# Griffin layer on one core: three tiles for r, i and the states of a chain step, and another place for the squared decay

## The chip, the core and the metric

The kernel runs on one core of a Trainium2 chip, in float32. The metric is the device time of one execution in microseconds (us). TensorE (PE) multiplies, ScalarE (ACT) runs activations and copies, VectorE (DVE) elementwise work and the scans, GpSimd (POOL) and SyncE (SP) issue DMA transfers. Each engine works through its own list of instructions in order; across engines they wait on semaphores.

## What is computed

One Griffin layer on 1024 tokens of width 2048, then a gated embedding. Cut to what matters (`proj[..., :2048]` is the branch that is convolved, the other half the gate):

```python
u = rmsnorm(h, norm_pre)
proj = u @ w_in                              # 2048 -> 4096
xb, gate = proj[..., :2048], proj[..., 2048:]
xc = causal_conv_width4(xb, conv_w) + conv_b # per channel
r = sigmoid(blockdiag(xc, w_r) + b_r)        # 8 blocks of 256 channels
i = sigmoid(blockdiag(xc, w_i) + b_i)
log_a = -8 * r * softplus(-lam)
a = exp(log_a)
b = sqrt(-expm1(2 * log_a)) * (i * xc)
h_t = a_t * h_{t-1} + b_t                    # scan over the tokens
y = (h * silu(gate)) @ w_out
h = h + rmsnorm(y, norm_post)
h = h + sigmoid(h @ w_gate) * (p @ w_ple)
```

## The kernel before, in words

**Matrix products.** Channels lie on the 128 partitions and tokens on the free axis, in two halves of 512 tokens (h=0 and h=1). Each float32 product is made of three matmuls of rounded parts (`mm3`): high weight by high operand (line 116), high by low (117), low by high (118). ACT makes a high part by a copy (106), DVE the low part by a subtraction (107). Weights are split so one product ahead of their use, into one of three places (`wp`, names whi_ and wlo_). The three large matrices go by Strassen's scheme: seven products m1 to m7 for each pair of output blocks, each a unit of 24 matmuls. A name such as x14m5 is product m5 of block 14 of w_in. Some weight tiles are sums, which a DMA that adds makes ahead of the product; GpSimd issues it (423).

**Where the chain stands.** While w_in's products run, the recurrent part runs between them, in eight blocks n of 256 channels, for h=0 some 5.4 units apart and for h=1 four products apart. A block has these steps:

- `block_conv`: one ACT instruction for each 128 channels starts xc (280), three DVE instructions each add a tap (283), and xc is split into a high and a low part in the tile x2 (106, 107).
- `block_ri`: one unit of 24 matmuls, r and i of the block, with a weight tile of its own (whi_ri, wlo_ri).
- `chain`: sigmoids for R and I (310, 311), I times xc (312), a tanh into Q (314), an exponential in place of R (318), squared three times: twice in place (319, 320) and once into A2 (321). Then Q = (A2 + 1) * Q on DVE (322), its root on ACT (323), I times Q (324), and the scan (328), which writes the states over Q. For h=0 the states are stored to memory, four units later; for h=1 they are multiplied with the gate into g (335), and g is stored four units later. Sigmoid and tanh, the exponential and the root each need another function table on ACT, so table loads stand between them.

**Places.** The pool named chain has one place for each tag, except two for the tag xb (the convolution's input). xc has 4 KB per partition, x2 8 KB (high and low part), rq 12 KB (R, I and Q in one tile). A2 is written over xc. A tile that takes a place waits until every reader of the tile before it has finished.

**Order.** SP and GpSimd issue in the order of the program text. PE, ACT and DVE get theirs from a scheduler that sees the program's order and the places, so that a change of places can reorder these three. In program order the convolution of block n+1 comes behind chain n for h=0; for h=1 it comes ahead of the matmuls of ri n, because there it is put two products behind a start that moves by four, and the matmuls six.

Of the kernel before, what the change touches and what calls it, by code (L numbers as in the profile page):

```python
# [9 lines left out]
F32R = mybir.dt.float32r  # L10
AF = mybir.ActivationFunctionType
ALU = mybir.AluOpType

P = 128
D = 2048
S = 1024
T = 512
# [17 lines left out]
def trunk_kernel(ctx, tc, xT, pT, par, w_in, w_ri, w_out, w_gate, w_ple, out):  # L35
    nc = tc.nc
# [11 lines left out]
    def bank(name):  # L48
        return psum.tile([P, T], F32, tag="ps", name=name)
# [4 lines left out]
    def chain_tile(tag, name, shape=(P, 2, T), dtype=F32, bufs=1):  # L54

        return pools["a"].tile(list(shape), dtype, tag=tag, name=name, bufs=bufs)
# [16 lines left out]
    def col(base, i):  # L73
        return cst[:, base + i : base + i + 1]
# [30 lines left out]
    def split(hi, lo, src):  # L105
        nc.scalar.activation(hi, src, AF.Copy)  # L106
        nc.vector.tensor_tensor(lo, src, hi.bitcast(F32), ALU.subtract)  # L107
# [7 lines left out]
    def mm3(ps, whi, wlo, ahi, alo, start, stop, more=False):  # L115
        nc.tensor.matmul(ps, whi, ahi, start=start, stop=False, skip_group_check=more)  # L116
        nc.tensor.matmul(ps, whi, alo, start=False, stop=False, skip_group_check=more)  # L117
        nc.tensor.matmul(ps, wlo, ahi, start=False, stop=stop, skip_group_check=more)  # L118
# [36 lines left out]
    st = {}  # L155
# [32 lines left out]
    def put(key, d, src, k=1):  # L188

        n_spills[0] += 1  # L190
        name = f"sp{n_spills[0]}"

        def store():
            t = spill(name, src.shape)
            nc.gpsimd.dma_start(t, src)  # L195
            d[key] = t

        later(k, store)
# [70 lines left out]
    def block_conv(h, n):  # L269
        xbp = st.pop(("xbp", h, n))  # L270
        c = slice(2 * n, 2 * n + 2)
        if h == 0:
            nc.vector.memset(xbp[:, :, 0:3], 0.0)
            nc.vector.tensor_copy(xcar[:, c, :], xbp[:, :, T : T + 3])
        else:
            nc.vector.tensor_copy(xbp[:, :, 0:3], xcar[:, c, :])
        xc = chain_tile("xc", f"xc{h}_{n}")
        for s in range(2):
            ct = 2 * n + s
            nc.scalar.activation(xc[:, s], xbp[:, s, 3 : T + 3], AF.Identity, bias=col(C_CB, ct),  # L280
                                 scale=col(C_CW + 48, ct))
            for j in (2, 1, 0):
                nc.vector.scalar_tensor_tensor(xc[:, s], xbp[:, s, j : j + T], col(C_CW + 16 * j, ct), xc[:, s],  # L283
                                               op0=ALU.mult, op1=ALU.add)
        x2 = chain_tile("x2", f"x2{h}_{n}", (P, 2, 2, T), F32R)
        split(x2[:, 0], x2[:, 1], xc)
        st["xc", h, n], st["x2", h, n] = xc, x2

    def block_ri(h, n):
        plain(w_ri[n], f"ri{h}_{n}", lambda u: mm_ri(h, n, u.pop("w")))  # L290

    def mm_ri(h, n, w):
        hi, lo = w
        x2 = st.pop(("x2", h, n))
        banks = [[bank(f"ri{h}_{n}_{a}{b}") for b in range(2)] for a in range(2)]
        for ri in range(2):
            for dd in range(2):
                for k in range(2):
                    c0 = ri * 512 + k * 256 + dd * P
                    mm3(banks[ri][dd], hi[:, c0 : c0 + P], lo[:, c0 : c0 + P], x2[:, 0, k], x2[:, 1, k],  # L300
                        k == 0, k == 1)
        chain(h, n, banks)

    def chain(h, n, banks):
        rq = chain_tile("rq", f"rq{h}_{n}", (P, 3, 2, T))
        R, I, Q = (rq[:, j] for j in range(3))
        A2 = st.pop(("xc", h, n))
        for s in range(2):
            ct = 2 * n + s
            nc.scalar.activation(R[:, s], banks[0][s], AF.Sigmoid, bias=col(C_BR, ct))  # L310
            nc.scalar.activation(I[:, s], banks[1][s], AF.Sigmoid, bias=col(C_BI, ct))
        nc.vector.tensor_tensor(I, I, A2, ALU.mult)
        for s in range(2):
            nc.scalar.activation(Q[:, s], R[:, s], AF.Tanh, scale=dk[:, 0, 2 * n + s : 2 * n + s + 1])

        for s in range(2):
            ct = 2 * n + s
            nc.scalar.activation(R[:, s], R[:, s], AF.Exp, scale=dk[:, 1, ct : ct + 1])
        nc.scalar.activation(R, R, AF.Square)
        nc.scalar.activation(R, R, AF.Square)  # L320
        nc.scalar.activation(A2, R, AF.Square)
        nc.vector.scalar_tensor_tensor(Q, A2, 1.0, Q, op0=ALU.add, op1=ALU.mult)
        nc.scalar.activation(Q, Q, AF.Sqrt)
        nc.vector.tensor_tensor(I, I, Q, ALU.mult)
        for s in range(2):
            ct = 2 * n + s
            init = 0.0 if h == 0 else hcar[:, ct : ct + 1]
            nc.vector.tensor_tensor_scan(Q[:, s], R[:, s], I[:, s], init, ALU.mult, ALU.add)
        if h == 0:
            nc.vector.tensor_copy(hcar[:, 2 * n : 2 * n + 2], Q[:, :, T - 1])  # L330
            for s in range(2):
                put(2 * n + s, hs, Q[:, s], 4)
        else:
            g = gs.pop(n)
            nc.vector.tensor_tensor(g, Q, g, ALU.mult)  # L335
            for s in range(2):
                put((("b12", "b22")[s], n), yd, g[:, s], 4)
# [484 lines left out]
    for h in range(NH):  # L822
        for n in range(NB):
            o = o2 - 4 + int(5.4 * n) if h == 0 else o3 + 5 + int(4.1 * n)
            if h == 0:
                at(o, lambda n=n: block_load(n))
            at(o + 2, lambda h=h, n=n: block_conv(h, n))
            at(o + 6, lambda h=h, n=n: block_ri(h, n), True)
# [138 lines left out]
```

## Time and profile before

| | us |
|---|---|
| median of 3 runs | 1428.23 |
| lowest and highest of them | 1427.18 and 1430.15 |
| the profiled execution | 1433.68 |
| its span, as the profile shows it | 1431.9 |
| PE busy in it | 1386.0 (97%) |
| DVE, ACT, POOL busy | 975.1, 720.3, 272.5 |

The profiled execution is 5.45 us longer than the median, and 1.78 us of it lie outside the span. The chain in h=0 stands between about 200 and 560 us of the span, the one in h=1 between about 570 and 820. In a row of the timeline, the time in brackets is how long the engine stood idle before it, and the name behind the arrow what ended that. The profile leaves out the numbers in names: x is the high or low part of xc, x0m any product of block 0, rq any block's tile.

### The profile page before, as it was taken

The numbers are of one execution on the slowest core, as the hardware profiler recorded it, in microseconds if no ns is written. First come the engines' busy times: TensorE is split into PE (matmuls) and PEld (weight loads), VectorE is DVE, ScalarE is ACT, GpSimd is POOL, SyncE is SP. The second block draws the span as 40 slices with busy tenths as digits, with TensorE's granted clock in tenths as the row PEclk, the third lists the DMA queues.
The fourth block names the chain that finished last, engine by engine and source line by source line (L and its number), as shares of the span: only waits on it lengthen the run. The fifth ranks groups of instructions, "written<-read, shape, count | busy, mean of one in ns | idle before, by whom it ended". The sixth has DMA issues, their size and how long they took to land.

```text
span 1431.9 us, 17158 instructions
## 1 busy us (share of the span) xinstructions
PE 1386.0 (97%) x6025; PEld 1132.2 (79%) x6025; DVE 975.1 (68%) x1299; ACT 720.3 (50%) x935; POOL 272.5 (19%) x422
## 2 busy tenths in 40 slices
PE   9999898999999999999999989999999999999997
PEld 6888676888888888877777868888787887788886
DVE  7587866666666566788899864364479695535786
ACT  8331247767577343788887752242335333323332
POOL 0012322112221110111102421100342132210021
PEclk9999999999999999999999999999999999999999
DMA  9778998687866897577867999771899599987995
GB/s 350 239 236 286 294 325 240 177 210 188 214 168 173 234 320 242 163 217 216 228 226 267 341 328 278 175 198 44 289 359 360 196 360 351 290 205 198 291 347 200
DMA packets 125815, 358.81 MB, mean 251 GB/s; under 512 B 15904, under 2 KB 16288, under 8 KB 125728
## 3 DMA queue, kind: packets, MB, share of 16 engines
q1 hardware_dynamic: 83232, 210.88, 41.8%
q0 software_dynamic: 42496, 146.83, 40.0%
q8 instruction: 47, 0.77, 0.2%
q14 instruction: 40, 0.33, 0.1%
HBM read 277.95 MB, written 79.69 MB: 250 GB/s over the span
## 4 chain that ended last, share of the span: by engine, by line
PE 55%; issue 13%; DMA 12%; DVE 10%; ACT 6%; POOL 3%; SPq 0%; POOLq 0%; DVEq 0%; ACTq 0%
PE xm L118 8%; PE xm L116 8%; PE xm L117 8%; PE hm L118 4%; PE hm L116 4%; PE hm L117 4%; PE ym L118 4%; PE ym L117 4%; PE ym L116 4%; POOL sp L195 2%; DVE xc L283 2%; PE ri L116 1%; PE ri L117 1%; PE ri L118 1%; DMA fhb<-sp 1%
## 5 line engine op out<-in xcount | busy, mean ns | idle before, releaser
L283 DVE SCALAR_TENSOR_TENSOR xc<-xbp,cst,xc 128x512 f32<-128x512 f32 x96 | 67.1, 745 | 0.3 <-ACT xc L280 0.2
L423 POOL DMA_DIRECT2D x_m<-in_w_in x64 | 57.6, 1013 | 30.4 <-DVE wlo_x15m L107 11.9
L195 POOL DMA_DIRECT2D sp<-g x32 | 17.5, 550 | 215.0 <-DVE g L592 157.1
L116 PE MATMUL ri<-x,whi_ri 128*128 128x512 f32 x128 | 49.6, 416 | 8.0 <-ACT x L106 8.0
L117 PE MATMUL ri<-x,whi_ri 128*128 128x512 f32 x128 | 51.1, 399 | 0.0
L118 PE MATMUL ri<-x,wlo_ri 128*128 128x512 f32 x128 | 50.7, 396 | 0.0
L725 POOL DMA_DIRECT2D out_t<-sg x32 | 17.6, 549 | 147.2 <-DVE sg L724 146.6
L423 POOL DMA_DIRECT2D y_m<-in_w_out x32 | 29.0, 955 | 79.3 <-DVE wlo_y7m L107 19.0
L423 POOL DMA_DIRECT2D h_m<-in_w_gate x32 | 29.0, 952 | 78.3 <-DVE wlo_h7m L107 19.6
L116 PEld LDWEIGHTS ri<-x,whi_ri 128*128 128x128 f32 x128 | 24.4, 193 | 15.7 <-ACT x L106 10.1
L195 POOL DMA_DIRECT2D sp<-ux x16 | 9.2, 574 | 144.3 <-DVE ux L585 120.2
L310 ACT ACT_TABLE_LOAD x14 | 18.0, 1283 | 27.0 <-DVE g L335 26.9
L106 ACT ACTIVATE x<-xc 128x1024 fp32r<-128x1024 f32 x16 | 16.9, 1055 | 24.9 <-DVE xc L283 24.9
L117 PEld LDWEIGHTS ri<-x,whi_ri 128*128 128x128 f32 x128 | 24.4, 190 | 6.3 <-DVE x L107 0.4
L118 PEld LDWEIGHTS ri<-x,wlo_ri 128*128 128x128 f32 x128 | 24.4, 191 | 5.9
L280 ACT ACTIVATE xc<-xbp,cst 128x512 f32<-128x512 f32 x32 | 24.4, 806 | 8.5 <-DMA xbp<-sp 7.5
L106 ACT ACTIVATE x_t<-xu 128x512 fp32r<-128x512 f32 x8 | 5.1, 632 | 45.8 <-DVE xu L349 45.8
L116 PE MATMUL pp<-p,whi_ple 128*128 128x512 f32 x64 | 25.1, 394 | 2.0 <-ACT p L106 2.0
L195 POOL DMA_DIRECT2D sp<-xb x16 | 8.7, 546 | 91.3 <-DVE xb L560 90.9
L195 POOL DMA_DIRECT2D sp<-z x16 | 8.7, 546 | 90.6 <-DVE z L621 58.5
L702 ACT ACTIVATE pp<-pp 128x512 f32<-128x512 f32 x16 | 9.4, 595 | 31.6 <-DMA sp<-pp 21.2
L118 PE MATMUL pp<-p,wlo_ple 128*128 128x512 f32 x64 | 24.9, 390 | 0.0
(722 smaller groups left out, 4963.1 us busy)
## 6 DMA issues: line engine op xcount, KB each, us to landing
x_m<-in_w_in SPq DMA_DIRECT2D x72, 512.0 KB, 5.5
x_m<-in_w_in POOLq DMA_DIRECT2D x64, 512.0 KB, 8.3
y_m<-in_w_out SPq DMA_DIRECT2D x40, 512.0 KB, 6.5
h_m<-in_w_gate SPq DMA_DIRECT2D x40, 512.0 KB, 9.5
y_m<-in_w_out POOLq DMA_DIRECT2D x32, 512.0 KB, 9.4
o<-sp SPq DMA_DIRECT2D x64, 256.0 KB, 8.9
h_m<-in_w_gate POOLq DMA_DIRECT2D x32, 512.0 KB, 9.1
raw_ri<-in_w_ri SPq DMA_DIRECT2D x16, 512.0 KB, 6.7
```

The lines of the kernel that those rows point to most:

```text
L106: nc.scalar.activation(hi, src, AF.Copy)
L116: nc.tensor.matmul(ps, whi, ahi, start=start, stop=False, skip_group_check=more)
L117: nc.tensor.matmul(ps, whi, alo, start=False, stop=False, skip_group_check=more)
L118: nc.tensor.matmul(ps, wlo, ahi, start=False, stop=stop, skip_group_check=more)
L195: nc.gpsimd.dma_start(t, src)
L280: nc.scalar.activation(xc[:, s], xbp[:, s, 3 : T + 3], AF.Identity, bias=col(C_CB, ct), scale=col(C_CW + 48, ct))
L283: nc.vector.scalar_tensor_tensor(xc[:, s], xbp[:, s, j : j + T], col(C_CW + 16 * j, ct), xc[:, s], op0=ALU.mult, op1=ALU.add)
L310: nc.scalar.activation(R[:, s], banks[0][s], AF.Sigmoid, bias=col(C_BR, ct))
L423: nc.gpsimd.dma_start(u["raw"], w[(p, *ADDED[name])], accum_op=ALU.add)
L702: nc.scalar.activation(t, b, AF.Copy)
L725: later(1, lambda: nc.gpsimd.dma_start(out[h, :, dt, :], sg))
```

## The change

```diff
@@ block_conv
-        x2 = chain_tile("x2", f"x2{h}_{n}", (P, 2, 2, T), F32R)
-        split(x2[:, 0], x2[:, 1], xc)
-        st["xc", h, n], st["x2", h, n] = xc, x2
+        hi, lo = (chain_tile(t, f"{t}{h}_{n}", dtype=F32R) for t in ("xhi", "xlo"))
+        split(hi, lo, xc)
+        st["xc", h, n], st["x2", h, n] = xc, (hi, lo)
@@ mm_ri
-                    mm3(banks[ri][dd], hi[:, c0 : c0 + P], lo[:, c0 : c0 + P], x2[:, 0, k], x2[:, 1, k],
+                    mm3(banks[ri][dd], hi[:, c0 : c0 + P], lo[:, c0 : c0 + P], x2[0][:, k], x2[1][:, k],
@@ chain
-        rq = chain_tile("rq", f"rq{h}_{n}", (P, 3, 2, T))
-        R, I, Q = (rq[:, j] for j in range(3))
-        A2 = st.pop(("xc", h, n))
+        R, I, Q = (chain_tile(t, f"{t}{h}_{n}") for t in ("rr", "ri", "rq"))
+        A2, xc = chain_tile("xlo", f"a2{h}_{n}"), st.pop(("xc", h, n))
...
-        nc.vector.tensor_tensor(I, I, A2, ALU.mult)
+        nc.vector.tensor_tensor(I, I, xc, ALU.mult)
```

R, I and Q become three tiles (rr, ri, rq; 4 KB each), the two parts of xc two tiles (xhi, xlo; 4 KB each), and A2 takes the place of xlo, not that of xc. The pool stays at 24 KB for these. No instruction is added or taken away: 1299 on DVE, 935 on ACT and as many table loads stand in both. SP's and GpSimd's lists are the same word for word but for numbers. From line 312 on, the lines of the kernel after are one lower. Three of the places at which the order of ACT and DVE differs follow.

**DVE, h=0, chain 0 and convolution 1.** Before, from the row of (A2 + 1) * Q on; wlo_x0m3 is the low part for the next Strassen product, x_b its operand, L328 the scan:

```order
L322 SCALAR_TENSOR_TENSOR rq0_0_1867<-xc0_0_1629,rq0_0_1867 128x1024
L388 SCALAR_TENSOR_TENSOR x_b224_1982<-fxb224_1929,x_b224_1982 128x512
L582 TENSOR_TENSOR ux0_1724<-xm6_0_1954,ux0_1724 128x512
L581 TENSOR_TENSOR ux1_1915<-ux1_1915,rstd_x0_578 128x512
L583 TENSOR_TENSOR ux0_1724<-ux0_1724 128x512
L324 TENSOR_TENSOR rq0_0_1867<-rq0_0_1867 128x1024
L283 SCALAR_TENSOR_TENSOR xc0_1_1934<-xbp0_1_1781,cst_80,xc0_1_1934 128x512
L328 SCALAR_TENSOR_TENSOR rq0_0_1867<-rq0_0_1867 128x512 x2
L283 SCALAR_TENSOR_TENSOR xc0_1_1934<-xbp0_1_1781,cst_80,xc0_1_1934 128x512
L330 COPY hcar_89<-rq0_0_1867 128x2
L283 SCALAR_TENSOR_TENSOR xc0_1_1934<-xbp0_1_1781,cst_80,xc0_1_1934 128x512 x3
L107 TENSOR_TENSOR wlo_x0m3_1951<-x0_m7_1334,whi_x0m3_1950 128x1024
```

After, from the same row on (L321 now); three taps of convolution 1 stand ahead of this piece, between I times xc and wlo_x1m6:

```order
L321 SCALAR_TENSOR_TENSOR rq0_0_1870<-a20_0_1871,rq0_0_1870 128x1024
L283 SCALAR_TENSOR_TENSOR xc0_1_1938<-xbp0_1_1782,cst_80,xc0_1_1938 128x512
L581 TENSOR_TENSOR ux0_1725<-xm6_0_1959,ux0_1725 128x512
L283 SCALAR_TENSOR_TENSOR xc0_1_1938<-xbp0_1_1782,cst_80,xc0_1_1938 128x512
L582 TENSOR_TENSOR ux0_1725<-ux0_1725 128x512
L283 SCALAR_TENSOR_TENSOR xc0_1_1938<-xbp0_1_1782,cst_80,xc0_1_1938 128x512
L323 TENSOR_TENSOR ri0_0_1869<-ri0_0_1869,rq0_0_1870 128x1024
L107 TENSOR_TENSOR wlo_x0m3_1956<-x0_m7_1334,whi_x0m3_1955 128x1024
L327 SCALAR_TENSOR_TENSOR rq0_0_1870<-rr0_0_1868,ri0_0_1869 128x512 x2
L107 TENSOR_TENSOR xlo0_1_1948<-xc0_1_1938,xhi0_1_1947 128x1024
L329 COPY hcar_89<-rq0_0_1870 128x2
L387 SCALAR_TENSOR_TENSOR x_b224_1987<-fxb224_1933,x_b224_1987 128x512
```

The convolution moved ahead of I times Q, wlo_x0m3 ahead of the scan, and x_b224 behind the scan and xlo.

**ACT, h=1, the end of chain 2 beside ri 3.** Before (a table load and the root of chain 2, L323, stand ahead of the split x21_3, on which ri 3 waits):

```order
L106 ACTIVATE whi_ri1_3_5105<-raw_ri1_3_5062 128x1024
L321 ACTIVATE xc1_2_4763<-rq1_2_5039 128x1024
L590 ACTIVATE xm4_11_5109<-g0_11_5134 128x512
L106 ACTIVATE y_b110_5139<-fyb110_5102 128x512
L106 ACTIVATE y_b111_5142<-fyb110_5102 128x512
L280 ACTIVATE xc1_3_4991<-xbp1_3_4869,cst_80 128x512 x2
L323 ACT_TABLE_LOAD
L323 ACTIVATE rq1_2_5039<-rq1_2_5039 128x1024
L106 ACTIVATE whi_x10m5_5150<-x10_m5_4954 128x1024
L106 ACTIVATE whi_x13m4_5196<-x13_m4_5147 128x1024
L106 ACTIVATE x21_3_5000<-xc1_3_4991 128x1024
```

After, the end of chain 2 and the sigmoids of chain 3 (L309, L310):

```order
L320 ACTIVATE a21_2_5084<-rr1_2_5081 128x1024
L589 ACTIVATE xm4_12_5245<-g0_12_5270 128x512
L106 ACTIVATE whi_x11m5_5299<-x11_m5_5109 128x1024
L322 ACT_TABLE_LOAD
L322 ACTIVATE rq1_2_5083<-rq1_2_5083 128x1024
L106 ACTIVATE whi_x14m4_5362<-x14_m4_5297 128x1024
L309 ACT_TABLE_LOAD
L309 ACTIVATE rr1_3_5331<-ri1_3_00_5303,cst_80 128x512
L310 ACTIVATE ri1_3_5332<-ri1_3_10_5305,cst_80 128x512
L309 ACTIVATE rr1_3_5331<-ri1_3_01_5304,cst_80 128x512
L310 ACTIVATE ri1_3_5332<-ri1_3_11_5306,cst_80 128x512
```

The last square of chain 2, a21_2, moved behind the split xhi1_3 (nine rows ahead of this piece); ACT holds it until the last low-part matmul (117) of ri 3, whose xlo it replaces.

**ACT, h=1, around whi_x14m5.** Before, chain 4:

```order
L106 ACTIVATE whi_x13m5_5491<-x13_m5_5310 128x1024
L310 ACTIVATE rq1_4_5523<-ri1_4_01_5496,cst_80 128x512
L311 ACTIVATE rq1_4_5523<-ri1_4_11_5498,cst_80 128x512
L590 ACTIVATE xm4_14_5446<-g0_14_5471 128x512
L314 ACTIVATE rq1_4_5523<-rq1_4_5523,dk_90 128x512 x2
L318 ACT_TABLE_LOAD
L318 ACTIVATE rq1_4_5523<-rq1_4_5523,dk_90 128x512 x2
L106 ACTIVATE whi_x14m5_5545<-x14_m5_5348 128x1024
```

After, the end of chain 3 and chain 4:

```order
L322 ACT_TABLE_LOAD
L322 ACTIVATE rq1_3_5333<-rq1_3_5333 128x1024
L309 ACT_TABLE_LOAD
L309 ACTIVATE rr1_4_5573<-ri1_4_00_5545,cst_80 128x512
L310 ACTIVATE ri1_4_5574<-ri1_4_10_5547,cst_80 128x512
L309 ACTIVATE rr1_4_5573<-ri1_4_01_5546,cst_80 128x512
L310 ACTIVATE ri1_4_5574<-ri1_4_11_5548,cst_80 128x512
L313 ACTIVATE rq1_4_5575<-rr1_4_5573,dk_90 128x512 x2
L317 ACT_TABLE_LOAD
L317 ACTIVATE rr1_4_5573<-rr1_4_5573,dk_90 128x512
L280 ACTIVATE xc1_5_5526<-xbp1_5_5392,cst_80 128x512 x2
L317 ACTIVATE rr1_4_5573<-rr1_4_5573,dk_90 128x512
L106 ACTIVATE whi_x14m5_5598<-x14_m5_5397 128x1024
```

Before, whi_x14m5 follows the two exponentials of chain 4; now the square and root of chain 3 and the convolution of block 5 (L280) come ahead of it as well.

## Rows read from the trace of the kernel before

**Rows 1.** The page: busy time of each engine, share of the span, instructions.

```profile
PE 1386.0 (97%) x6025; PEld 1132.2 (79%) x6025; DVE 975.1 (68%) x1299; ACT 720.3 (50%) x935; POOL 272.5 (19%) x422
```

**Rows 2.** PE's waits: line, releaser, us in total, times, longest.

```profile
PE ri L116 <- ACT x L106: 8.0, 5, 2.8
PE xm L118 <- DVE wlo_x0m L107: 6.3, 2, 5.6
...
PE xm L116 <- ACT whi_x14m L106: 2.7, 1, 2.7
```

**Rows 3.** 250 to 560 us: length, busy us of PE, PEld, DVE, ACT, POOL; PEclk, DMA.

```profile
250.00:560.00 310.00, 310.00 (x1365) 255.71 (x1364) 199.05 (x244) 181.87 (x215) 55.03 (x74) 1.00 0.79 212
```

**Rows 4.** Timeline of PE, h=1: start, us, instruction, count [idle before, releaser].

```profile
571.26 0.39 PE L116 MATMUL ri<-x,whi_ri 128*128 128x512 f32 x1
...
582.32 0.39 PE L116 MATMUL xm<-x_t,whi_x7m 128*128 128x512 f32 x1
...
587.76 0.39 PE L116 MATMUL xm<-x_t,whi_x5m 128*128 128x512 f32 x1
...
629.04 1.88 PE L116 MATMUL ri<-x,whi_ri 128*128 128x512 f32 x4 [2.84 <-ACT x L106]
...
780.26 1.09 PE L116 MATMUL ri<-x,whi_ri 128*128 128x512 f32 x4
```

**Rows 5.** Timeline of PE, h=0, product x0m3 and the start of ri 1.

```profile
231.06 0.40 PE L117 MATMUL xm<-x_b,whi_x0m 128*128 128x512 f32 x1
237.01 0.79 PE L118 MATMUL xm<-x_b,wlo_x0m 128*128 128x512 f32 x1 [5.56 <-DVE wlo_x0m L107]
...
243.60 0.39 PE L116 MATMUL ri<-x,whi_ri 128*128 128x512 f32 x1
```

**Rows 6.** Timeline of DVE, h=0, chain 0 and convolution 1.

```profile
218.94 1.22 DVE L312 TENSOR_TENSOR rq<-rq,xc 128x1024 f32<-128x1024 f32 x1
223.06 1.23 DVE L107 TENSOR_TENSOR wlo_x1m<-x_m,whi_x1m 128x1024 fp32r<-128x1024 f32 x1 [2.90 <-ACT whi_x1m L106]
225.44 1.23 DVE L322 SCALAR_TENSOR_TENSOR rq<-xc,rq 128x1024 f32<-128x1024 f32 x1 [1.15 <-ACT xc L321]
226.59 0.68 DVE L388 SCALAR_TENSOR_TENSOR x_b<-fxb,x_b 128x512 fp32r<-128x512 f32 x1
...
230.12 0.74 DVE L283 SCALAR_TENSOR_TENSOR xc<-xbp,cst,xc 128x512 f32<-128x512 f32 x1
...
233.75 2.07 DVE L283 SCALAR_TENSOR_TENSOR xc<-xbp,cst,xc 128x512 f32<-128x512 f32 x3
235.74 1.22 DVE L107 TENSOR_TENSOR wlo_x0m<-x_m,whi_x0m 128x1024 fp32r<-128x1024 f32 x1
```

**Rows 7.** Timeline of ACT, h=0, the same stretch.

```profile
219.66 1.34 ACT L318 ACTIVATE rq<-rq,dk 128x512 f32<-128x512 f32 x2
...
224.36 1.05 ACT L321 ACTIVATE xc<-rq 128x1024 f32<-128x1024 f32 x1
```

**Rows 8.** Timeline of ACT, h=1, chain 2.

```profile
634.96 1.28 ACT L310 ACT_TABLE_LOAD   x1 [5.97 <-DVE g L335]
636.25 0.69 ACT L310 ACTIVATE rq<-ri,cst 128x512 f32<-128x512 f32 x1
...
650.18 1.04 ACT L321 ACTIVATE xc<-rq 128x1024 f32<-128x1024 f32 x1
...
652.71 1.52 ACT L280 ACTIVATE xc<-xbp,cst 128x512 f32<-128x512 f32 x2
```

**Rows 9.** Timeline of DVE, h=1, convolution 3 and the scan of chain 2.

```profile
653.79 4.06 DVE L283 SCALAR_TENSOR_TENSOR xc<-xbp,cst,xc 128x512 f32<-128x512 f32 x6
...
661.27 2.45 DVE L328 TENSOR_TENSOR_SCAN rq<-rq,hcar 128x512 f32<-128x512 f32 x2
```

**Rows 10.** Timeline of GpSimd, h=1: the store of g of block 3.

```profile
697.03 1.09 POOL L195 DMA_DIRECT2D sp<-g  x2 [10.16 <-DVE g L335]
```

**Rows 11.** The page: DMA issues, count, KB each, us from issue to landing.

```profile
x_m<-in_w_in POOLq DMA_DIRECT2D x64, 512.0 KB, 8.3
```

## The prediction

> **What bounds the kernel now.** First the page's busy times: PE works 97% of the span, DVE 68%, ACT 50% [rows 1]. So a gain can come only out of the 3% in which PE stands, and out of the time after a stand in which it is slow. Next, PE's waits by line: of those that the chain has a part in, the first matmuls of the ri units wait 8.0 us for the high part of xc, the low part of a product of block 0 costs one wait of 5.6 us, and x14m5 one of 2.7 us [rows 2]. Then the timeline, to see what a wait really costs. In h=1 ri 0 starts at 571.26 and ri 7 at 780.26, 209.0 us apart [rows 4]. Between two of them stand four products of 5.44 us (582.32 to 587.76) and a ri unit that I take at 5.5: 27.3 us a period, 191.1 for seven, so 17.9 us are lost there, more than twice the sum that the waits show for ri. Part of the difference is the wait for x14m5; another is that four matmuls after a wait take 1.88 us, and 1.09 without one [rows 4]. In h=0 between 250 and 560 us PE is busy every microsecond [rows 3]: there only the start can gain, where the low part of x0m3 is late (PE stops at 231.06 and goes on at 237.01 [rows 5]).
>
> **Part 1, the names alone.** No instruction is added or removed, the pool is as large as before, and SP and GpSimd keep their order. Splitting one tile into three changes only which wait ends when. A sigmoid of the next chain no longer waits for g or the store that reads Q; it waits for the scan and for I times Q. In h=1 the g step is 1.22 us long, and ACT stood 5.97 us ahead of the sigmoids' table load, waiting for it [rows 8]. At most about 1.2 us a period could come from this, if nothing else moved.
>
> **Part 2, xc is free earlier (h=0).** Before, xc is held until (A2 + 1) * Q, now until I times xc, which ends at 218.94 + 1.22 = 220.16 [rows 6]. Convolution 1 therefore goes ahead of the end of chain 0. I lay DVE's new order with the old durations. ACT's exponentials end at 221.0 [rows 7], the first convolution instruction takes 0.76 (half of 1.52 [rows 8]), the three taps 2.07 [rows 6]: 223.8. wlo_x1m6 then ends at 225.05 where it ended at 224.29; ACT's high part is later by the same 0.76. A2 ends 0.76 later than 224.36 + 1.05 [rows 7], at 226.15; (A2 + 1) * Q at 227.4; three taps and two steps of ux, at a pitch of 0.6 to 0.7, at 230.6; I times Q at 231.8; wlo_x0m3 at 233.0. Before, it ended at 235.74 + 1.22 = 236.96, so PE goes on 4.0 us earlier. But x_b224, the low part of that product's own operand, was done by 227.27 before [rows 6] and now stands behind the scan (2.45 [rows 9]) and xlo (1.22): about 237.3. Three more parts of the same product follow it, with wlo_ri among them, to about 240.3. PE needs x_b224 some 3 us after it goes on, at 236, so it stands again, in pieces, and ends the product at about 240.8 where ri 1 started at 243.60 [rows 5]. That leaves 2.8 us of the 4.0; 0.3 goes for the later wlo_x1m6. I take **-2.5 us**; the bounds are -5 (the x_b parts cost nothing) and +1 (they cost all of it and the later wlo_x1m6 besides). The rest of h=0 I cost at nothing: PE never waits there, and the low parts of weights stand no later against the taps than before; what hides the moves is the lead of one product on each weight, 5.44 us.
>
> **Part 3, A2 in the place of xlo (h=1).** Here the convolution of block n+1 comes first in program order, so that xlo n+1 gets the place and A2 of chain n has to wait until the last low-part matmul of ri n+1. That adds a wait, on ACT, which holds its whole list; the end of chain n, and with it the place of R, moves behind ri n+1. From that point E the way to the next ri is, with the durations before: A2 1.04 [rows 8], (A2 + 1) * Q 1.22 to 2.3; then four half-size DVE steps at 0.6 and wlo_x11m5 to 5.9; I times Q to 7.1; wlo_x14m4, whose place comes free when the product behind ri ends (E + 5.4), to 8.3; the scan 2.45 to 10.7 [rows 9]; the sigmoids' table 1.29 (634.96 to 636.25 [rows 8]) to 12.0; four sigmoids at a pitch of 0.6 to 14.4; tanh 1.3 to 15.7; a table to 17.0; one exponential 0.7 to 17.7; the convolution's first half 0.76 to 18.4; six taps 4.06 to 22.5 [rows 9]. ACT has meanwhile the second half, an exponential, a table, a gate, a square and whi_ri, to about 23.7; the high part of xc is there at 24.7 and the low one at 25.9. PE has finished its four products at 21.8 and has four matmuls to do with the high part alone (1.1): it loses about 3.0, and 0.3 to 0.8 for the slow matmuls after the wait. I take 3.4. Before, five periods from ri 2 to ri 7 took (780.26 - 629.04) / 5 = 30.2 each [rows 4], a loss of 2.9. So the old wait goes and one of nearly the same size takes its place. The first two periods start with slack (chain 0 has no late chain ahead of it): I give 0, 0.6 and 2 to the first three, 3.4 to the fourth and the sixth, 1 to the last, in which w_in's products run out and ACT has less to split.
>
> The fifth is special. The DMA that completes x14m5's weight stands on GpSimd behind the store of g of block 3, which already waits for that g before (697.03, after 10.16 us of idle [rows 10]). g 3 now ends at about E + 12, the two stores take 1.1 us of issuing, the transfer 8.3 [rows 11]: it lands at E + 21, and ACT, busy with chain 4 and convolution 5 until 20, makes the high part by 22 and DVE the low one by 23.3. PE wants it after three products, at E + 16.3: a stand of 5 to 6.5, with the slow matmuls some 6.8, where it was 2.7 [rows 2]. ri 5 is covered by it. The sum is 0 + 0.6 + 2 + 3.4 + 6.8 + 3.4 + 1 = 17.2 against 17.9: **-0.7 us**. The bounds are -11 (only x14m5's wait is left) and +10 (the way from E two microseconds longer in four periods, and x14m5 later by two more).
>
> **Part 4, the end of h=1.** g of block 7 comes some 5 us later, and its store with it; two loads of the next phase read it, while the scheduler now puts the first weight of that phase ahead of the last split of an operand. I leave it at 0, between -3 and +3.
>
> The sum is -2.5 - 0.7 + 0 = -3.2 us: 1430.5 for the profiled execution of 1433.68, and for the median, from which that execution stands 5.45 us off for reasons that the change doesn't touch, 1428.2 - 3.2 = **1425.0 us**.
>
> **Rule against row.** A switch of ACT's table costs 1.29 us here from the load's start to the next activation [rows 8]; the sum uses that. The Trainium skill (ScalarE: Activation LUTs, What ACT_TABLE_LOAD costs) states 1283 ns for the load and about 1380 ns more of drain. By it the two switches on the way from E would add an estimated 2.7 us a period, some 11 over four, and the time would be near 1436, rival C's; the row bears out the load and shows no drain ahead of the activation, though a drain before the load could hide in idle time.
>
> **The rivals.** *B, the ri waits go altogether.* The scan in chain n might come before wlo_x14m4, or the operations I have queued ahead of I times Q find gaps: three microseconds less from E and ri never waits. Then only x14m5's 6.8 of the 17.9 stays: -11 - 2.5 gives about 1414.5. For it: DVE is idle for a third of the span [rows 1]. Against: it is in order, and the scan can't start before the product behind ri ends. *C, slower: the new wait on ACT makes the way from E the longest in every period.* It decides where the four periods that the way from E can bind (the third, fourth, sixth and seventh) lose 0.8 more than I gave each, so 4.2 where I have 3.4. Two microseconds more in four periods and one or two more at x14m5 are +10; less the 2.5 of h=0 about +7: 1435. For it: ACT is held at A2 with splits of weights queued behind it, and each of these makes PE wait. Against: at E PE has its next weights split already. *D, nothing to measure.* The change frees xc sooner but adds no place, and where I have a gain the parts of x_b give it back; the waits of ri stay as they are: 1428. In a sentence of its own: the Trainium skill (Perfetto Trace Analysis, Optimization Strategy) reads consistent bubbles as a possible lack of SBUF for the next tile; the ri waits are such bubbles, 24 KB before and after, and by that rule they would stay, which is D's side, while the rows can't show it.
>
> **How the numbers follow.** About 0.2% (2.9 us, 1425.4 to 1431.1) can be told from no change. The forecast, 1425.0 with a range of its own from 1421 to 1429, gets 0.38; it stands at the edge, so 0.22 of that is faster, 0.14 same, 0.02 slower. B 0.18, all faster. C 0.25, of which 0.24 slower. D 0.19: 0.02 faster, 0.16 same, 0.01 slower. Faster 0.42, same 0.31, slower 0.27. A range from 1412 to 1437 leaves out the lower third of B and a good third of C, 0.15 to 0.2 in all; it holds the bounds of parts 2 and 4, and part 3's with them but for the corners where all lie on one side.
>
> **What would show it.** Right: x0m3's wait shorter and broken into pieces; ACT idle ahead of the last square of each chain in h=1, released by ri's low-part matmul; ri 0 to ri 7 within a microsecond or two of 209; x14m5's wait at 5 to 6.5. Wrong: ri without waits (B), periods over 31 us (C), or x0m3 as late as before (D). The forecast fails too if the loads of x_b land at another time than here, since all of part 2 hangs on them.

## The result, and the profile after

The changed kernel is slower: 1448.54 us in the median of four runs (1444.70 to 1453.13) against 1428.42 (1427.18 to 1430.15), a ratio of 1.0136 with a 95% interval from 1.0118 to 1.0155. The forecast was 1425.0. Its profiled execution took 1453.13 us with a span of 1451.3, which is 19.4 us more than the span before.

The page of the kernel after shows the engines as busy as before (busy us, share, instructions); PE's 5.7 us more are matmuls that ran slower:

```profile
PE 1391.7 (96%) x6025; PEld 1133.8 (78%) x6025; DVE 977.0 (67%) x1299; ACT 719.4 (50%) x935; POOL 273.3 (19%) x422
```

So the time went into waits. PE's waits, kernel after (line, releaser, us in total, times, longest), to be read against [rows 2]:

```profile
PE ri L116 <- ACT xhi L106: 15.7, 5, 7.4
PE xm L116 <- ACT whi_x14m L106: 6.9, 2, 4.2
PE ym L116 <- ACT whi_y0m L106: 6.8, 2, 4.2
...
PE xm L118 <- DVE wlo_x0m L107: 2.1, 2, 1.4
...
PE xm L117 <- DVE x_b L387: 1.9, 2, 1.2
```

The row of wlo_x0m holds two products of block 0; x0m3 alone waits 1.44 us instead of 5.56, with the new wait for x_b beside it: the gain in h=0 is there. The ri units wait 15.7 us instead of 8.0. The rows of whi_x14m hold more than one product too. The 2.7 us of [rows 2] are not x14m5's: they stand at another product of block 14, at 157.25, and x14m5 starts without a wait in the kernel before (PE's timeline, kernel before):

```profile
157.25 0.50 PE L116 MATMUL xm<-x,whi_x14m 128*128 128x512 f32 x1 [2.69 <-ACT whi_x14m L106]
...
714.18 0.39 PE L116 MATMUL xm<-x_t,whi_x14m 128*128 128x512 f32 x1
```

So x14m5 now waits 4.15 us for its high part and 1.81 for its low part, 5.96 in all, where it waited for nothing. PE's timeline of the kernel after tells where (start, us, instruction, idle before and its releaser):

```profile
231.57 0.50 PE L118 MATMUL xm<-x_b,wlo_x0m 128*128 128x512 f32 x1 [1.44 <-DVE wlo_x0m L107]
...
235.61 0.50 PE L117 MATMUL xm<-x_b,whi_x0m 128*128 128x512 f32 x1 [1.23 <-DVE x_b L387]
...
237.95 0.50 PE L117 MATMUL xm<-x_b,whi_x0m 128*128 128x512 f32 x1 [0.69 <-DVE x_b L387]
...
239.22 0.39 PE L116 MATMUL ri<-xhi,whi_ri 128*128 128x512 f32 x1
...
566.88 0.39 PE L116 MATMUL ri<-xhi,whi_ri 128*128 128x512 f32 x1
...
622.50 1.20 PE L116 MATMUL ri<-xhi,whi_ri 128*128 128x512 f32 x4 [0.70 <-ACT xhi L106]
...
658.10 2.07 PE L116 MATMUL ri<-xhi,whi_ri 128*128 128x512 f32 x4 [7.38 <-ACT xhi L106]
...
693.23 2.07 PE L116 MATMUL ri<-xhi,whi_ri 128*128 128x512 f32 x4 [4.76 <-ACT xhi L106]
...
721.87 0.58 PE L116 MATMUL xm<-x_t,whi_x14m 128*128 128x512 f32 x1 [4.15 <-ACT whi_x14m L106]
724.69 0.80 PE L118 MATMUL xm<-x_t,wlo_x14m 128*128 128x512 f32 x1 [1.81 <-DVE wlo_x14m L107]
...
791.77 1.19 PE L116 MATMUL ri<-xhi,whi_ri 128*128 128x512 f32 x4 [0.34 <-ACT xhi L106]
```

Three stretches make up the 19.4 us. ri 0 of h=1 starts at 566.88 where it was 571.26 [rows 4]: 4.4 us won, and ri 1 of h=0 (239.22 against 243.60 [rows 5]) shows that they were won ahead of ri 1. From there to ri 7 it takes 224.9 us instead of 209.0: 15.9 lost. From ri 7 to the end of the span it takes 659.5 us instead of 651.6 (1431.9 - 780.26): 7.9 lost.

ACT in the period from ri 2 to ri 3 shows the new wait that was forecast, and one that was not (timeline of ACT, kernel after; a is A2):

```profile
628.80 1.06 ACT L320 ACTIVATE a<-rr 128x1024 f32<-128x1024 f32 x1 [2.51 <-PE ri L117]
629.77 0.58 ACT L589 ACTIVATE xm<-g 128x512 f32<-128x512 f32 x1
635.58 1.06 ACT L106 ACTIVATE whi_x9m<-x_m 128x1024 fp32r<-128x1024 f32 x1 [5.23 <-DMA x_m<-in_w_in]
636.66 1.28 ACT L322 ACT_TABLE_LOAD   x1
637.95 1.06 ACT L322 ACTIVATE rq<-rq 128x1024 f32<-128x1024 f32 x1
...
643.32 1.28 ACT L309 ACT_TABLE_LOAD   x1 [3.36 <-DVE rq L327]
```

A2 waits for the last low-part matmul of ri 2, as predicted. Then ACT stands 5.23 us at the split of x9m5, whose DMA has not landed, and the root of chain 1 stands behind that split in ACT's list. GpSimd, which issues that DMA, in the same stretch:

```profile
611.13 1.63 POOL L195 DMA_DIRECT2D sp<-g  x3 [18.95 <-DVE g L334]
612.76 0.95 POOL L422 DMA_DIRECT2D x_m<-in_w_in  x1
626.10 0.56 POOL L195 DMA_DIRECT2D sp<-g  x1 [12.39 <-DVE g L591]
626.73 0.88 POOL L422 DMA_DIRECT2D x_m<-in_w_in  x1
```

The DMA for x9m5 leaves at 626.73, right behind a store that GpSimd had waited 12.39 us to issue, and lands at 635.56. DVE's gate product holds GpSimd, GpSimd holds the weight, the weight holds ACT, and ACT holds the chain.

The kernel before has the same store and the same DMA in the same order, and loses nothing by them (ACT, then GpSimd, kernel before; ri 2 starts at 629.04 there [rows 4]):

```profile
625.06 1.06 ACT L323 ACTIVATE rq<-rq 128x1024 f32<-128x1024 f32 x1
...
637.88 1.05 ACT L106 ACTIVATE whi_x9m<-x_m 128x1024 fp32r<-128x1024 f32 x1
```

```profile
630.57 0.88 POOL L423 DMA_DIRECT2D x_m<-in_w_in  x1
```

There the root of chain 1 has run ahead of ri 2, the DMA leaves 1.5 us behind the start of ri 2 and lands 7.1 us behind it, and the split comes later and does not wait. In the kernel after the DMA leaves 4.2 us behind the start of ri 2 and lands 13.1 us behind it, and the root stands behind the split.

### The profile page after: what moved, and what is told of

Its sections match the earlier page's. It is cut to its first block, busy times and chain, and to the rows that moved or that the text cites. A ratio compares the mean times of both kernels' runs of the same rounds, so it can differ in the third digit from the quotient of the medians.

```text
span 1451.3 us, 17153 instructions
## 1 busy us (share of the span) xinstructions
PE 1391.7 (96%) x6025; PEld 1133.8 (78%) x6025; DVE 977.0 (67%) x1299; ACT 719.4 (50%) x935; POOL 273.3 (19%) x422
## 4 chain that ended last, share of the span: by engine, by line
PE 50%; issue 19%; DMA 14%; DVE 6%; ACT 6%; POOL 4%; SPq 1%; POOLq 0%; DVEq 0%; ACTq 0%
PE xm L118 8%; PE xm L117 8%; PE xm L116 8%; PE ym L118 4%; PE ym L116 4%; PE ym L117 4%; PE hm L118 3%; PE hm L116 3%; PE hm L117 3%; POOL sp L195 3%; DMA y_m<-in_w_out 2%; PE ri L117 2%; PE ri L118 2%; PE ri L116 2%; DMA fyb<-sp 2%
## 5 line engine op out<-in xcount | busy, mean ns | idle before, releaser
L116 PE MATMUL ri<-xhi,whi_ri 128*128 128x512 f32 x128 | 51.4, 422 | 15.7 <-ACT xhi L106 15.7
L117 PE MATMUL ri<-xlo,whi_ri 128*128 128x512 f32 x128 | 53.2, 416 | 0.8 <-DVE xlo L107 0.8
L118 PE MATMUL ri<-xhi,wlo_ri 128*128 128x512 f32 x128 | 52.7, 412 | 0.0
L422 POOL DMA_DIRECT2D y_m<-in_w_out x32 | 29.3, 951 | 90.5 <-DVE wlo_y7m L107 19.0
L724 POOL DMA_DIRECT2D out_t<-sg x32 | 17.6, 551 | 147.4 <-DVE sg L723 146.8
L116 PEld LDWEIGHTS ri<-xhi,whi_ri 128*128 128x128 f32 x128 | 25.4, 202 | 23.6 <-ACT xhi L106 17.8
L117 PEld LDWEIGHTS ri<-xlo,whi_ri 128*128 128x128 f32 x128 | 25.6, 200 | 8.4 <-DVE xlo L107 2.2
L118 PEld LDWEIGHTS ri<-xhi,wlo_ri 128*128 128x128 f32 x128 | 25.4, 198 | 6.2
L321 DVE SCALAR_TENSOR_TENSOR rq<-a,rq 128x1024 f32<-128x1024 f32 x16 | 19.6, 1224 | 14.6 <-ACT a L320 14.5
L280 ACT ACTIVATE xc<-xbp,cst 128x512 f32<-128x512 f32 x32 | 25.0, 802 | 7.6 <-DMA xbp<-sp 7.6
L309 ACT ACT_TABLE_LOAD x15 | 19.2, 1283 | 16.6 <-DVE rq L327 16.5
L320 ACT ACTIVATE a<-rr 128x1024 f32<-128x1024 f32 x16 | 16.8, 1053 | 20.6 <-PE ri L117 14.5
L323 DVE TENSOR_TENSOR ri<-ri,rq 128x1024 f32<-128x1024 f32 x16 | 19.6, 1224 | 8.9 <-ACT rq L322 8.7
```

The source lines that it names most:

```text
L422: nc.gpsimd.dma_start(u["raw"], w[(p, *ADDED[name])], accum_op=ALU.add)
L724: later(1, lambda: nc.gpsimd.dma_start(out[h, :, dt, :], sg))
```

## The experiments

Theory 1 was that A2's wait makes the loss; theories 2 and 4 blame the three tiles or the early convolution, theory 5 the late DMA; theory 3 doubts that the gain of h=0 lasts, and theory 6 concerns the 8 us behind ri 7. "Periods" are the distances between starts of ri units in h=1, from PE's timeline.

**The three tiles alone.**

```diff
 # the kernel before, with only this
-        rq = chain_tile("rq", f"rq{h}_{n}", (P, 3, 2, T))
-        R, I, Q = (rq[:, j] for j in range(3))
+        R, I, Q = (chain_tile(t, f"{t}{h}_{n}") for t in ("rr", "ri", "rq"))
```

> The three tiles rr, ri, rq alone; the two parts of xc stay one tile and A2 stays over xc. Theory 1 (the loss of the changed kernel is A2's wait for the matmuls of the next block in h=1, and nothing else): the order of convolution and chain stays as in the kernel before, ri 0 to ri 7 in h=1 takes 203 to 209 us, x0m3's low part is as late as before (near 236), time 1422 to 1429 us. Theory 2 (the sigmoids, which come earlier with tiles of their own, push work of PE's weights back on ACT): ri 0 to ri 7 over 215 us, time over 1438 us.

Measured: 1422.44 us, ratio 0.9956 (0.9941 to 0.9970). x0m3 is as late as before, ri 0 to ri 7 takes 206.6 us, and ri 7 to the end 647.9. PE's timeline of this kernel:

```profile
237.06 0.79 PE L118 MATMUL xm<-x_b,wlo_x0m 128*128 128x512 f32 x1 [4.90 <-DVE wlo_x0m L107]
```

Theory 2 falls: the tiles are a gain of some 6 us by themselves. And the gain at x0m3 needs A2 out of xc: ri 1 of h=0 starts at 244.09 here, and at 239.09 in the next run, which has A2 out of xc and R, I and Q in one tile.

**A2 in xlo's place, with R, I and Q one tile.**

```diff
 # the changed kernel, with this
-        R, I, Q = (chain_tile(t, f"{t}{h}_{n}") for t in ("rr", "ri", "rq"))
+        rq = chain_tile("rq", f"rq{h}_{n}", (P, 3, 2, T))
+        R, I, Q = (rq[:, j] for j in range(3))
```

> A2 in the place of xlo and xc as two split parts, but R, I and Q stay one tile. Theory 1: A2 waits for the last low-part matmul of the next ri in h=1 as in the changed kernel, ri 0 to ri 7 takes 222 us or more, and since the sigmoids wait for g as well, 1446 to 1455 us. Theory 2 (the sigmoids of their own tiles do the harm): ri 0 to ri 7 near 209, time 1420 to 1428 us, the gain of h=0 included.

Measured: 1453.12 us, ratio 1.0166 (1.0146 to 1.0186); ri 0 to ri 7 takes 229.7 us. The loss comes with A2's place.

**A2 in xlo's place for h=0, over xc for h=1.**

```diff
 # the changed kernel, with this
-        A2, xc = chain_tile("xlo", f"a2{h}_{n}"), st.pop(("xc", h, n))
+        xc = st.pop(("xc", h, n))
+        A2 = chain_tile("xlo", f"a2{h}_{n}") if h == 0 else xc
```

> The whole change for h=0, but A2 over xc for h=1. Theory 1: ri 0 of h=1 starts 4 to 5 us earlier than before (571.3), as in the changed kernel, and ri 0 to ri 7 takes 203 to 209 us: 1417 to 1425 us. Theory 3 (the stretch from ri 0 on only gives back what the transfers make it give back, because w_in's weights arrive no earlier): ri 7 at 780 as before, 1426 to 1430 us.

Measured: 1415.93 us, ratio 0.9908 (0.9888 to 0.9928). ri 0 to ri 7 takes 204.3 us, where the changed kernel, which differs in h=1 by this one place, takes 224.9. Theory 3 falls. PE's timeline of this kernel, with ri 0, the two waits over 1 us that ri has left, and ri 7:

```profile
562.92 0.39 PE L116 MATMUL ri<-xhi,whi_ri 128*128 128x512 f32 x1
...
647.07 1.20 PE L116 MATMUL ri<-xhi,whi_ri 128*128 128x512 f32 x4 [1.14 <-ACT xhi L106]
...
707.08 2.08 PE L116 MATMUL ri<-xhi,whi_ri 128*128 128x512 f32 x4 [3.73 <-ACT xhi L106]
...
767.24 0.40 PE L116 MATMUL ri<-xhi,whi_ri 128*128 128x512 f32 x1
```

**The convolution one product later in h=1.**

```diff
 # the changed kernel, with this
-            at(o + 2, lambda h=h, n=n: block_conv(h, n))
+            at(o + 2 + h, lambda h=h, n=n: block_conv(h, n))
```

> The changed kernel, with the convolution of block n+1 put one product later for h=1, so that it stands behind the matmuls of ri n in program order and A2 of chain n takes the place of xlo n before xlo n+1 does. Theory 1 (A2's wait makes the loss): the last squares in h=1 wait for no matmul of the next block, ri 0 to ri 7 takes 195 to 209 us, time 1408 to 1425 us. Theory 4 (the loss is that the convolution, freed early, goes ahead of the chain on DVE and ACT): ri 0 to ri 7 stays over 218 us, time over 1440 us.

Measured: 1436.94 us, ratio 1.0043 (1.0020 to 1.0067), ri 0 to ri 7 220.8 us: between both theories. A2's wait is gone, but the edit moved more than that. ACT's timeline of this kernel:

```profile
637.01 1.28 ACT L589 ACT_TABLE_LOAD   x1
638.30 0.60 ACT L589 ACTIVATE xm<-g 128x512 f32<-128x512 f32 x1
640.28 1.06 ACT L106 ACTIVATE whi_x9m<-x_m 128x1024 fp32r<-128x1024 f32 x1 [1.37 <-DMA x_m<-in_w_in]
641.35 1.28 ACT L317 ACT_TABLE_LOAD   x1
...
648.77 1.04 ACT L320 ACTIVATE a<-rr 128x1024 f32<-128x1024 f32 x1
```

A2 is squared without a wait, but a gate and a split stand between the two exponentials, with two more table loads, and ACT waits for x9m5 here too. This run decides nothing between theories 1 and 4; it showed that the late weight is not A2's alone.

**The DMA for the m5 products one product earlier.**

```diff
 # the changed kernel, with this
-            stages += [(7, LOAD, load), (5, ADD, add)]
+            stages += [(7, LOAD, load), (6 if (key, name) == ("x", "m5") else 5, ADD, add)]
```

> The changed kernel, with the DMA that completes the weight of each m5 product of w_in issued one product earlier, so that on GpSimd it stands ahead of the store that it stood behind (x9m5, x11m5 and x13m5 ahead of a store of the gate product, x14m5 ahead of the two stores of g 3). Theory 5 (the way from A2 to the next ri is long because ACT stands, ahead of the root, at the split of a weight whose DMA is late): the idle times ahead of the splits of x9m5 (5.2 us), x11m5 (3.1) and x13m5 (1.8) go, the periods from ri 2 to ri 4 fall from 35 to 31 or 32 us, that from ri 4 to ri 5 from 38.6 to 31 to 33, 1432 to 1440 us. Rival (the way is long without that wait, and ACT only waits where it has time): the periods stay at 34 or more, 1445 to 1450 us.

Measured: 1429.14 us, ratio 0.9989 (0.9970 to 1.0007). One position in GpSimd's list, for the DMA of each m5 product, is worth some 19 us. ACT's timeline of this kernel, the same place as above:

```profile
627.23 1.06 ACT L320 ACTIVATE a<-rr 128x1024 f32<-128x1024 f32 x1 [2.51 <-PE ri L117]
628.20 1.04 ACT L106 ACTIVATE whi_x9m<-x_m 128x1024 fp32r<-128x1024 f32 x1
629.14 0.58 ACT L589 ACTIVATE xm<-g 128x512 f32<-128x512 f32 x1
629.74 1.28 ACT L322 ACT_TABLE_LOAD   x1
631.04 1.06 ACT L322 ACTIVATE rq<-rq 128x1024 f32<-128x1024 f32 x1
...
636.40 1.28 ACT L309 ACT_TABLE_LOAD   x1 [2.65 <-DVE rq L327]
```

A2 waits for ri's matmul as long as before (2.51), so that wait stays; the split behind it does not wait, and the sigmoids' table load comes 9.2 us behind A2 instead of 14.5. The periods are 30.3, 31.9 and 32.0 where they were 35.6, 35.1 and 38.6, and ri 0 to ri 7 takes 208.5 us. Theory 5 holds.

**The same without x14m5.**

```diff
 # the changed kernel, with this
-            stages += [(7, LOAD, load), (5, ADD, add)]
+            stages += [(7, LOAD, load), (6 if (key, name) == ("x", "m5") and p != 14 else 5, ADD, add)]
```

> The changed kernel with the earlier DMA for all m5 products but x14m5's, which stays behind the stores of g 3. Theory 5, by its two parts: the periods from ri 2 to ri 4 fall to 30 to 32 us as with the whole edit; the period from ri 4 to ri 5 keeps x14m5's wait of 4 to 6 us and stays at 35 to 38, so ri 0 to ri 7 is near 213 us and the time 1431 to 1438 us. Rival (x14m5's lateness followed from the two long periods ahead of it): it goes too, ri 0 to ri 7 near 208 and 1426 to 1431 us.

Measured: 1436.36 us, ratio 1.0042 (1.0018 to 1.0066); periods 30.3, 30.7 and 35.4, ri 0 to ri 7 212.0 us. PE's timeline of this kernel:

```profile
705.73 0.50 PE L116 MATMUL xm<-x_t,whi_x14m 128*128 128x512 f32 x1 [2.81 <-ACT whi_x14m L106]
708.12 0.79 PE L118 MATMUL xm<-x_t,wlo_x14m 128*128 128x512 f32 x1 [1.53 <-DVE wlo_x14m L107]
```

x14m5's wait is its own, behind the stores of g 3, and needs no long period ahead of it: 4.3 us of waiting.

**A2 in PSUM.**

```diff
 # the changed kernel, with this
-        A2, xc = chain_tile("xlo", f"a2{h}_{n}"), st.pop(("xc", h, n))
+        xc = st.pop(("xc", h, n))
...
-        nc.scalar.activation(A2, R, AF.Square)
-        nc.vector.scalar_tensor_tensor(Q, A2, 1.0, Q, op0=ALU.add, op1=ALU.mult)
+        for s in range(2):
+            nc.scalar.activation(banks[0][s], R[:, s], AF.Square)
+            nc.vector.scalar_tensor_tensor(Q[:, s], banks[0][s], 1.0, Q[:, s], op0=ALU.add, op1=ALU.mult)
```

> The changed kernel with A2 in neither place: it is written, in two halves, over the two PSUM banks that held r's sums, which are free after the sigmoids. So xc is free after I times xc in both halves of the tokens, and A2 waits for nothing. Theory 1: ri 0 to ri 7 takes 193 to 206 us and the time is 1405 to 1420 us, as good as the kernel that keeps A2 over xc for h=1, or better. Theory 4 (xc free early is itself what hurts in h=1, since the convolution goes ahead of the chain): ri 0 to ri 7 over 212 us, 1425 us or more. Either way two PSUM banks are held some 12 us longer, which may make a product wait.

Measured: 1418.09 us, ratio 0.9920 (0.9892 to 0.9948), ri 0 to ri 7 203.2 us. Here the convolution goes early in h=1 too and hurts nothing: theory 4 falls. No ri unit waits for xc any more. PE now waits for low parts of weights instead (x12m4 1.94 us, x14m5 1.95, and 1.57 at one ri unit), and ACT still stands 5.26 us at x9m5, with sigmoids of chain 2 behind that split.

**A2 in PSUM, and the earlier DMA.** Both edits together.

> A2 in PSUM in both halves of the tokens (xc free early everywhere, A2 waits for nothing) and the earlier DMA for the m5 products. Theory 1 with theory 5: no ri waits over 1 us, the wait for the low part of x14m5 (1.95 us) goes, ri 0 to ri 7 197 to 202 us, 1408 to 1416 us. Rival (the PSUM kernel is held by DVE, not by its DMAs): 1415 to 1420 us.

Measured: 1405.73 us (1404.94 to 1407.30), ratio 0.9821 (0.9784 to 0.9858), faster than expected and the best of all. ri 0 to ri 7 takes 193.2 us: six periods of 27.4 and one of 28.9; the waits for low parts of x12m4 and x14m5 are gone. The window of 565 to 760 us in this kernel (length, busy us of PE, PEld, DVE, ACT, POOL, granted clock, DMA) and below that of 566 to 792 in the changed one:

```profile
565.00:760.00 195.00, 193.76 (x849) 159.02 (x848) 181.88 (x230) 180.78 (x227) 27.60 (x44) 1.00 0.75 234
```

```profile
566.00:792.00 226.00, 203.82 (x846) 164.04 (x845) 175.94 (x217) 169.94 (x210) 26.48 (x42) 0.94 0.64 198
```

The same matmuls (849 and 846 in the records) fit in 195 us instead of 226; of the 31 us, 21 are idle time of PE (226 - 203.82 against 195 - 193.76), and in the other 10 PE is busy for longer with the same work, at a granted clock of 0.94 in the mean against 1.00.

**The earlier DMA with A2 over xc in h=1.** The edits of the third and the fifth experiment together.

> The whole change for h=0, A2 over xc for h=1, and the earlier DMA for the m5 products of w_in. Theory 5 for this kernel: x14m5's and the like do not wait here, the store stands ahead of a DMA that has time, so within 3 us of the kernel without the earlier DMA (1415.9). Rival: the late chain shows there too and 3 to 8 us are won, 1408 to 1413 us.

Measured: 1415.58 us, ratio 0.9899 (0.9875 to 0.9923), ri 0 to ri 7 201.2 us. With A2 over xc in h=1, the place of the DMA is worth nothing that can be told (1415.93 without it). The four kernels together, in us:

| | A2 over xc in h=1 | A2 in xlo's place in h=1 |
|---|---|---|
| DMA of m5 as it was | 1415.93 | 1448.54 |
| DMA of m5 earlier | 1415.58 | 1429.14 |

The late DMA costs 19 us with A2 in xlo's place and nothing with A2 over xc; with A2 in PSUM, where sigmoids stand behind the split, it costs 12 (1418.09 against 1405.73). And A2's wait is not free once the DMA is in time: it still costs 13.6 us, 7.3 of them between ri 0 and ri 7 in the profiles (208.5 against 201.2).

**One single late end, ahead of the y phase,** run twice.

```diff
 # the kernel with A2 in xlo's place for h=0, with this
-        A2 = chain_tile("xlo", f"a2{h}_{n}") if h == 0 else xc
+        A2 = chain_tile("xlo", f"a2{h}_{n}") if h == 0 or n == 6 else xc
```

> The whole change for h=0, A2 over xc for h=1, but for block 6 of h=1 in xlo's place as in the changed kernel: one single late end of a chain, right ahead of the y phase. Theory 6 (the 8 us that the changed kernel loses behind ri 7 come from g 6 and g 7, which are late against ri 7): ri 0 to ri 7 near 205 to 208, and 3 to 8 us more from ri 7 to the end than the 647.2 us of the kernel with A2 over xc throughout h=1; 1419 to 1427 us. Rival (they come from something else): under 2 us more, 1415 to 1418 us.

> The kernel with one single late end of a chain (block 6) once more, for a second profile. Theory 6: ri 7 to the end again 3 us or more over the 647.2 us of the kernel without it. Rival (accident): within 2 us of 647.2. The spread of its executions (1418 to 1432 us) lets both be possible in one look; the two profiles together count.

Measured: 1428.73 us (1418.11 to 1431.96) and 1427.90 (1423.14 to 1434.12), against 1415.93 without the late end. ri 0 to ri 7 stays at 204.2 and 205.6 us; ri 7 to the end takes 652.2 and 659.6 instead of 647.2. The place of one tile in one block costs some 12 us by the medians, 10 by the ratios. The second of these profiles shows, on GpSimd (g 6, then g 7) and on PE:

```profile
785.15 1.08 POOL L195 DMA_DIRECT2D sp<-g  x2 [19.06 <-DVE g L335]
805.49 1.09 POOL L195 DMA_DIRECT2D sp<-g  x2 [9.92 <-DVE g L335]
```

```profile
862.62 0.79 PE L116 MATMUL ym<-y_b,whi_y0m 128*128 128x512 f32 x1 [5.19 <-ACT whi_y0m L106]
```

GpSimd stands 19.06 us for g 6, with stores of the y phase behind it. The kernel without the late end issues g 6 here:

```profile
772.47 1.08 POOL L195 DMA_DIRECT2D sp<-g  x2 [11.90 <-DVE g L335]
```

That is 5.2 us behind ri 7, where the kernel with the late end has 16.3. g 7 comes later too, 36.6 us behind ri 7 instead of 27.8, so these two runs do not tell g 6 from g 7.

**The changed kernel once more.**

> The changed kernel once more, for a second profile. Theory 6 (the 8 us lost behind ri 7 come with g 6 and g 7, late against ri 7): ri 7 to the end again 656 us or more where the kernel before has 651.6. Rival (they were an accident of that execution's transfers): 650 to 654 us, and a faster execution. ri 0 to ri 7 within 2 us of 224.9 under either.

Measured: 1447.38 us, ratio 1.0114 (1.0073 to 1.0154). ri 0 to ri 7 takes 225.5 us, ri 7 to the end 654.7 us, between the two expectations. The seven profiles of kernels with a late g 6 give 651.0 to 659.6 us behind ri 7, 656.1 in the mean; the seven others (with the kernel before) 644.8 to 651.6, 648.5 in the mean. Theory 6 holds in the mean, with 7.6 us, but not in each execution: the kernel with the earlier DMA has its g 6 as late and needs 651.0.

## Why the prediction was wrong, step by step

The span of the profiled execution grew by 19.4 us where the forecast had it fall by 3.2, a miss of 22.6: 16.6 of it between ri 0 and ri 7 of h=1 (224.9 against 208.3, part 3), 7.9 behind ri 7 (part 4), less 1.9 that h=0 won beyond the forecast (part 2).

**What bounds the kernel: right but for one row.** The wait of 2.7 us that was read as x14m5's is another product's, at 157.25; x14m5 waited for nothing before. The sum does not use it: it takes the old loss from the starts of the ri units and prices the new stand of x14m5 by itself.

**Part 1, the names alone: the bound holds, the term was left out.** It was bounded at 1.2 us a period and then put at nothing in the sum; the first experiment measured a gain of 6.3 us (1428.7 by the same ratio to 1422.4). In the profiles 2.4 of it lie between ri 0 and ri 7, and 3.7 behind ri 7, which is within the spread of the kernels there (644.8 to 651.6). With A2 in xlo's place the tiles gain 4.6 us (1453.12 to 1448.54). This miss hid a part of the others.

**Part 2, h=0: right, a size off.** -2.5 us was taken, -4.4 measured. The order of events is as laid: x0m3's low part early, two shorter stands at x_b (1.23 and 0.69 us), ri 1 at 239.22 where 240.8 was forecast. 1.2 of the difference is an earlier start: the exponentials of chain 0 run at 218.49 in the profile after and at 219.66 before [rows 7], behind a split of x_b that waits for a DMA. Over the twelve profiles with A2 out of xc in h=0, ri 1 starts between 233.7 and 239.2, but most of that spread is there at ri 0 already (195.2 to 199.9), ahead of the first chain; the two other kernels start ri 0 at 199.9 and 199.1. From ri 0 to ri 1 the twelve take 38.4 to 40.1 us, the two with A2 over xc 43.7 and 45.0: a gain of some 5 us. Their exponentials start 17.6 to 19.4 us behind ri 0, the two others' 19.8 and 20.6; why the loads of x_b land earlier stays open.

**Part 3, A2's wait: the mechanism right, one step wrong, and that step is more than half of the miss.** The forecast for ri 0 to ri 7 was 208.3 us. A2 waits for ri as forecast, and x14m5 stands 5.96 us where 5 to 6.5 was forecast. What failed is "wlo_x11m5 to 5.9": the splits on the way from E were given their own durations only, and no wait for the weight that they split. x14m5 was followed to its place on GpSimd, behind the store of g 3, and called special; x9m5, x11m5 and x13m5 stand there behind a store of their own that waits for DVE, and the prediction did not follow them. The sum, period by period in us:

| period | forecast | changed kernel | DMA earlier but for x14m5 | DMA earlier |
|---|---|---|---|---|
| ri 0 to 1 | 27.3 | 27.4 | 27.4 | 27.4 |
| ri 1 to 2 | 27.9 | 28.2 | 28.2 | 28.2 |
| ri 2 to 3 | 29.3 | 35.6 | 30.3 | 30.3 |
| ri 3 to 4 | 30.7 | 35.1 | 30.7 | 31.9 |
| ri 4 to 5 | 34.1 | 38.6 | 35.4 | 32.0 |
| ri 5 to 6 | 30.7 | 30.0 | 30.0 | 30.2 |
| ri 6 to 7 | 28.3 | 30.0 | 30.1 | 28.5 |
| sum | 208.3 | 224.9 | 212.0 | 208.5 |

The kernel with the DMA earlier but for x14m5 is the forecast's own picture (x14m5 late, the others not): 212.0, 3.7 us off in all. The step from it to the changed kernel, 12.9 us, is the one that was missing: 5.3, 4.4 and 3.2 in the three periods in which ACT stands at x9m5 (5.23 us), x11m5 (3.08) and x13m5 (1.78). That the kernel with all these DMAs earlier comes out at 208.5, next to the forecast, is luck: x14m5 does not wait there, and the forecast has it wait.

**Part 4, the end of h=1: wrong.** It was left at 0 between -3 and +3 and cost 7.9 us in the first profile, 3.0 in the second, some 7.6 in the mean over kernels. g 7 was seen to come some 5 us later (against ri 7 it comes 6.9 later), but g 6, 11.7 us later, was not, nor were the stores of the y phase that stand behind g 6 on GpSimd. The two runs with one late end show that such an end costs; whether by g 6, by g 7 or by the stores behind them is not shown, and which transfer decides between 651 and 660 us stays open. PE ends up waiting for whi_y0m, in the second run with one late end behind loads of y_b (fyb) that land late, in a stretch in which the profile shows the DMA engines busy all the time (a share of 1.05 from 840 to 880 us, in the kernel before and the one after alike). A run that moves those stores alone was not made.

**Rule against row.** The root's table load in the changed kernel starts at 636.66, behind an activation that ends at 636.64, and the next one starts at 637.95: 1.31 us from activation to activation. The Trainium skill (ScalarE: Activation LUTs, What ACT_TABLE_LOAD costs) states 1283 ns for the load, which the trace shows, and about 1380 ns of drain, which it does not show here. For the switch the row was right; the time came out on the side to which the rule pointed, but by the other causes above. The Trainium skill also says that consistent bubbles can mean that there is not enough SBUF or PSUM for the next tile (Perfetto Trace Analysis, Optimization Strategy). The kernels with A2 in PSUM agree: with a place for A2 that nothing else wants, no ri waits for xc, where the changed kernel has 15.7 us of such waits.

**The rivals.** C had the sign, at 0.25, and named "splits of weights queued behind it", but priced the way 2 us longer in four periods; the third, fourth and fifth period came out 4.4 to 6.3 us longer than forecast, the sixth and seventh -0.7 and 1.7, and ACT was held at the split itself, by its weight. B's outcome, that ri's waits go, can be had: the kernels with A2 in PSUM reach it by another place for A2, not by gaps on DVE.

## What to carry to other kernels

When a change puts a chain behind a wait on an in-order engine, follow every instruction that now stands between the chain's steps to its last releaser, a DMA's place in its issuing queue too, and not only the one that is known to be late. When a tile is to lie in another tile's place, ask whose last reader it then waits for in program order: A2 in xlo's place gave 12.5 us less, the tiles included, as long as it was done only in h=0, where that reader came early, and the kernel took 20 us more than before as soon as it was done in h=1 too, where it came late. A place that nothing else wants at that time, here two PSUM banks whose sums had been read, beat both once the weight's DMA was in time (1405.73 us); with the late DMA it did not beat A2 over xc in h=1 (1418.09 against 1415.93).

## What the runs showed of the hardware

A square written to PSUM and read there by DVE ran at 583 ns for 512 elements on ACT and 682 ns on DVE, in two halves; a chain kept ACT busy with it for 1.11 us and DVE for 1.29, against 1.05 and 1.22 for the whole in SBUF. So it costs under 0.1 us more on each engine, and no product was seen to wait for the banks.

A long wait of PE was paid twice here. After a wait of 4.8 or 7.4 us the next four matmuls took 2.07 us, after one of 0.7 us 1.20. The granted clock shows why: it is 0.50 from 658 to 661 us of the changed kernel, the lower of its two levels, behind the wait of 7.38 us, and 1.00, the upper one, from 622 to 625, behind that of 0.70 (windows, as above):

```profile
658.00:661.00 3.00, 2.90 (x7) 2.32 (x8) 2.95 (x5) 3.00 (x7) 0.00 (x0) 0.50 0.88 266
```

```profile
622.00:625.00 3.00, 2.19 (x8) 1.53 (x9) 3.00 (x4) 3.00 (x5) 0.00 (x0) 1.00 0.29 107
```

In the h=1 of the changed kernel some 10 us came on top of the waits in this way. At x0m3 the change removes it: before, the clock is 0.52 in the mean from 237.0 to 240.3 us, behind the stand of 5.56, and after, with three short stands, 1.00 from 231.5 to 239.2.
